# An encoder layer's output projection: by halves of 512 rows, seven products over the whole contraction, with sums of its weights made in the first pass

## The chip, the cores and the metric

The kernel runs on one core of a Trainium2 chip, as one program. The metric is the device time in microseconds (us), from three runs; what is compared is their median. One further execution was profiled. The engines are named as in the profile: PE is TensorE (PEld its weight loads), DVE VectorE, ACT ScalarE, POOL GpSimd, SP SyncE, which issues nearly all transfers in one queue, in order.

## The reference

One layer on x of 1024 rows by 2048 columns, in float32:

```python
h = rmsnorm(x, pre_g) * (1.0 + scale[:, None]) + shift[:, None]   # shift, scale, gate = silu(c) @ w_ada + b_ada
q, k, v, gate_a, u, gate_p = split(h @ w_in)                      # w_in 2048 x 4608
y_a = windowed_gqa(q, k, v, rel_table, sink) * silu(gate_a)       # 1024 x 1024
y_p = multiscale_pool(u, w_pool_grp, pool_scale) * silu(gate_p)   # 1024 x 1024
g_a, g_p = split(sigmoid(h @ w_merge + b_merge))                  # w_merge 2048 x 4096
merged = g_a * (y_a @ w_br_attn) + g_p * (y_p @ w_br_pool)        # 1024 x 2048
o = merged @ w_out                                                # w_out 2048 x 2048
out = x + gate[:, None] * rmsnorm(o, post_g)
```

The output projection is `merged @ w_out` with the last line.

## The kernel before, in words

Every float32 matmul is done as three: both operands are split in a high and a low part (`split`, lines 90 to 92: ACT copies the high part, DVE subtracts it to get the low one), and hi x hi, hi x lo and lo x hi are summed in PSUM. Operands lie with the contraction on the 128 partitions.

The big products go by Strassen's scheme in Winograd's form (`strassen`, lines 202 to 288). A block of four 128 x 512 results costs seven products, not eight, on sums of quarters: the moving side has B11, T3, T2, B21, T4, T1 and B22, the weights A11, S3, S2, A12, A22, S1 and S4. T and S are sums and differences. A *pair* is one call of `strassen`: seven products of twelve matmuls with 512 moving columns (line 227). Its PSUM banks are X, Z and V. ACT or DVE empties them into tiles p7, u2, u4 and c (lines 237, 265, 282; p7 is `p` in the profile), and `finish` takes each result block. `run` (line 313) steps through a pair and works off a list of side steps between the products; the last product of a pair is run inside the next one.

The stages, in the program's order: x is normalised and turned; pass 1 multiplies the first half of h's contraction with w_in and w_merge (first four pairs apart, then `pass1`, line 584; about 120 to 425 us for the pairs on w_in that have side steps which read w_ada for modulation and gate); pass 2 takes the second half, with attention and pooling between; two branch projections, b = 0 and b = 1 (loop from line 946); the output projection (from line 1012).

In a pair the weights come by `load_raws` (line 172 and on, the transfers at 179) into `raw` tiles of a pool of four, `wp`; whi and wlo, the split weights, have four buffers each. In the branch projections `fetch_gate` (972) loads a gate `gt` and applies the sigmoid, `finish` (984) multiplies each block by it. For b = 0 the block goes to memory (mp_d). For b = 1 the block of b = 0 is loaded and added, which makes m, the merged rows. The first eight 128-row tiles of the contraction of m stay in SBUF (`mr`), the others go to memory (m_d). The inputs y are tiles of a pool (`ysrc`) that is closed when b = 1 begins; the result tiles of b = 1 lie in the pool `ev4`, opened before `mr`.

The output projection has two parts. Four `out_pair`s (1068 to 1130) do the first half of the contraction by seven products, with 256 weight columns as the moving side (lines 1075, 1077, 1078); the four weight sums are made on DVE at that place; partial results go to memory (po_d). Then the second half of the contraction is done without the scheme, 512 columns at a time (lines 1164 to 1166), and each block gets its first sum from po_d, its sum of squares (ACT) and its scale (DVE, POOL); `finish_rows` (1190) puts x and the row's norm to it.

The order on each engine is set by the program's scheduler from the code's order and its waits; each engine then runs its list in that order. An instruction that waits holds all behind it on its engine.

## Time and profile before

| | |
|---|---|
| runs, median (lowest to highest) | 2163.88 us (2163.26 to 2164.78) |
| the profiled execution's own time | 2160.09 us |
| its span, first to last instruction | 2158.1 us |
| PE busy | 2121.3 us, 98% |
| DVE, ACT, POOL busy | 67%, 50%, 4% |
| output projection, first to last matmul | 1807.6 to 2149.6 us |
| granted PE clock over the span | 0.999 |
| transfers, mean | 190 GB/s |

A row of a group gives the line, engine, operation, output and inputs by name, shape, count, then busy time and mean ns of one, then idle time of the engine ahead of it and who ended it. A row of the timeline gives start, length, engine, line and what is done; in brackets the idle time ahead and its releaser. A row of the chain of waits gives start, length and what. A row of the waits view gives who waited for whom: us in total, times, longest. PE's pipelined matmuls overlap, so the mean ns of one is longer than the pitch.

### The profile page before, as it was taken

To read this page: it belongs to the slowest core of one execution; us is meant where nothing else is said; L and a number is where in the kernel's file an instruction comes from. 1 tells how busy PE (TensorE), PEld (TensorE's weight loads), DVE (VectorE), ACT (ScalarE), POOL (GpSimd) and SP (SyncE) were. 2 spreads that over 40 slices of the span, in tenths; PEclk is the share of its full clock that TensorE was granted. 3 is DMA by queue.
4 is the path that set the end of the run, shared out by engine and by line. 5 is a ranking of instruction groups with operands and counts; after the bars stand their busy time and mean duration, and the time that the engine had idled before them with its cause. 6 is when DMAs were issued, how large, how long until landed. Compare 5 with 4: busy or idle time off the path is not lost.

```text
span 2158.1 us, 29842 instructions
## 1 busy us (share of the span) xinstructions
PE 2121.3 (98%) x10335; PEld 1768.0 (82%) x10335; DVE 1449.1 (67%) x2558; ACT 1088.9 (50%) x2045; POOL 77.9 (4%) x113
## 2 busy tenths in 40 slices
PE   6999999999999999999999999999999999999998
PEld 3588888888888888888888888888788888999886
DVE  5786666665445767767777887657858878544456
ACT  5654444444474636677775333335546545444353
POOL 0000000000000000000000000000000000000363
PEclk9999999999999999999999999999999999999999
DMA  9985566664443355545545666755645654538455
GB/s 328 289 271 190 187 204 197 211 197 138 164 155 103 131 191 177 164 166 193 168 156 181 225 211 214 233 171 185 224 161 163 203 168 160 190 110 292 149 198 188
DMA packets 281655, 410.58 MB, mean 190 GB/s; under 512 B 21482, under 2 KB 158850, under 8 KB 281504
## 3 DMA queue, kind: packets, MB, share of 16 engines
q1 hardware_dynamic: 280048, 406.43, 57.4%
q0 software_dynamic: 1120, 2.19, 0.3%
q8 instruction: 81, 1.33, 0.3%
q14 instruction: 70, 0.57, 0.1%
q10 hardware_dynamic: 336, 0.06, 0.0%
HBM read 295.32 MB, written 115.37 MB: 190 GB/s over the span
## 4 chain that ended last, share of the span: by engine, by line
PE 89%; DVE 4%; DMA 3%; ACT 2%; issue 1%; SPq 0%; ACTq 0%; DVEq 0%
PE Z L227 29%; PE V L227 19%; PE X L227 19%; PE OUT L1166 3%; PE OUT L1165 3%; PE OUT L1164 3%; PE GEMV L444 1%; PE Z L1077 1%; PE Z L1078 1%; PE Z L1075 1%; DVE wlo L92 1%; PE XT L396 1%; DMA gt<-proj_d 1%; PE V L1078 1%; PE V L1075 1%
## 5 line engine op out<-in xcount | busy, mean ns | idle before, releaser
L91 ACT ACTIVATE whi<-raw 128x512 fp32r<-128x512 f32 (+1 forms) x584 | 356.2, 612 | 596.4 <-PE Z L227 279.6
L92 DVE TENSOR_TENSOR wlo<-raw,whi 128x512 fp32r<-128x512 f32 (+1 forms) x584 | 399.2, 687 | 292.0 <-PE Z L227 181.5
L95 DVE TENSOR_TENSOR u<-V,u 128x512 f32<-128x512 f32 x96 | 66.0, 688 | 53.3 <-PE V L227 48.2
L95 DVE TENSOR_TENSOR raw<-raw,raw 128x512 f32<-128x512 f32 x80 | 55.1, 688 | 61.9 <-DMA raw<-in_w_merge_dram 40.2
L227 PE MATMUL X<-B11h,whi 128*128 128x512 f32 x336 | 92.4, 393 | 1.3 <-ACT B11h L91 0.8
L227 PE MATMUL Z<-T1h,whi 128*128 128x512 f32 x336 | 92.1, 392 | 1.5 <-ACT T1h L91 1.5
L227 PE MATMUL V<-T4h,whi 128*128 128x512 f32 x336 | 92.3, 393 | 0.0
L227 PE MATMUL Z<-B22h,whi 128*128 128x512 f32 x336 | 92.2, 394 | 0.0
L227 PE MATMUL V<-T3h,whi 128*128 128x512 f32 x336 | 91.8, 392 | 0.0
L227 PE MATMUL X<-B11l,whi 128*128 128x512 f32 x336 | 91.3, 390 | 0.2 <-DVE B11l L92 0.2
L227 PE MATMUL Z<-T2h,whi 128*128 128x512 f32 x336 | 91.3, 391 | 0.0
L227 PE MATMUL X<-B21h,whi 128*128 128x512 f32 x336 | 90.9, 390 | 0.0
L227 PE MATMUL Z<-B22l,whi 128*128 128x512 f32 x336 | 90.9, 390 | 0.0
L227 PE MATMUL V<-T4l,whi 128*128 128x512 f32 x336 | 90.9, 390 | 0.0
L227 PE MATMUL Z<-T2h,wlo 128*128 128x512 f32 x336 | 90.9, 390 | 0.0
L227 PE MATMUL V<-T3l,whi 128*128 128x512 f32 x336 | 90.8, 390 | 0.0
L227 PE MATMUL V<-T4h,wlo 128*128 128x512 f32 x336 | 90.8, 390 | 0.0
L227 PE MATMUL Z<-T1l,whi 128*128 128x512 f32 x336 | 90.8, 390 | 0.0
L227 PE MATMUL Z<-T1h,wlo 128*128 128x512 f32 x336 | 90.7, 390 | 0.0
L227 PE MATMUL Z<-T2l,whi 128*128 128x512 f32 x336 | 90.7, 390 | 0.0
L227 PE MATMUL X<-B11h,wlo 128*128 128x512 f32 x336 | 90.6, 390 | 0.0
L227 PE MATMUL X<-B21l,whi 128*128 128x512 f32 x336 | 90.6, 390 | 0.0
(310 smaller groups left out, 5064.6 us busy)
## 6 DMA issues: line engine op xcount, KB each, us to landing
part<-part_d SPq DMA_DIRECT2D x136, 256.0 KB, 4.7
ada<-in_w_ada_dram SPq DMA_DIRECT2D x128, 256.0 KB, 4.4
raw<-in_w_in_dram SPq DMA_DIRECT2D x64, 512.0 KB, 4.0
raw<-in_w_merge_dram SPq DMA_DIRECT2D x64, 512.0 KB, 4.8
proj_d<-part SPq DMA_DIRECT2D x68, 256.0 KB, 2.1
gada<-in_w_ada_dram SPq DMA_DIRECT2D x32, 512.0 KB, 4.4
gt<-proj_d SPq DMA_DIRECT2D x64, 256.0 KB, 3.7
raw<-in_w_out_dram SPq DMA_DIRECT2D x32, 512.0 KB, 4.2
```

Source lines behind the costliest of these rows:

```text
L91: nc.scalar.activation(hi, src, AF.Copy)
L92: nc.vector.tensor_tensor(lo, src, f32(hi), ALU.subtract)
L95: (eng or nc.vector).tensor_tensor(o, a, b, ALU.add)
L227: nc.tensor.matmul(ps, w_[:, i], op[mov][j][m_], start=fresh and i == 0 and n == 0, stop=i == nj - 1 and n == 2, skip_group_check=True)
L396: nc.tensor.matmul(banks[j][:, m * P:(m + 1) * P], xts[4 * s + m, q][:, j * P:(j + 1) * P], turn[4 * s + m], start=True, stop=True)
L444: ins = nc.tensor.matmul(pv[g:g + 32, :], scz[:, kc, :], tile_of(kc), start=kc < 4, stop=kc >= 12, tile_position=(0, g))
L1075: nc.tensor.matmul(o_, hi[:, ts_], wh, start=fresh and t % 2 == 0 and j == 0, stop=False, skip_group_check=True)
L1077: nc.tensor.matmul(o_, hi[:, ts_], wl, start=False, stop=False, skip_group_check=True)
L1078: nc.tensor.matmul(o_, lo[:, ts_], wh, start=False, stop=j == KS - 1, skip_group_check=True)
L1164: nc.tensor.matmul(pb, hi[:, ts_], wh, start=fresh and k == KP[0], stop=False, skip_group_check=not fresh)
L1165: nc.tensor.matmul(pb, hi[:, ts_], wl, start=False, stop=False, skip_group_check=not fresh)
L1166: nc.tensor.matmul(pb, lo[:, ts_], wh, start=False, stop=k == KT - 1, skip_group_check=not fresh)
```

## The change

The output projection now goes by halves of 512 rows of x and, in each, by two blocks of 512 weight columns out of each half of w_out: four `out_pair`s of seven products over the whole contraction of 2048. Each product is 4 groups (JP) of 2 tiles, 2 banks (128 rows each), 3 matmuls: 48 matmuls, with 512 weight columns moving. The sums S1 to S4 of w_out's quarters are made during the first sixteen pairs of pass 1 (`weight_sums`: four loads of 256 KB with the pair's first product, four additions on DVE and four stores behind its sixth) and are stored in `ws_d`; the output projection loads them like plain weights. Result tiles in pass 1 go from 9 buffers to 6, and the sums have 6. In b = 1 the merged rows of half 0 stay in SBUF, those of half 1 go through m_d; `mr` is now opened before `ev4`, and `ev4` is closed before the output projection. The first half's first blocks go to memory (o_d). Work on half 0's rows is spread over the third and fourth `out_pair`; the last pair finishes rows 4 and 5 (of eight blocks of 128) behind its fifth product, and rows 6 and 7 at the end. POOL has no part in the stage.

```diff
@@ pass 1
+    ev = ev_ctx.enter_context(pool("ev1a", 6, side="right"))
+    wsp = ev_ctx.enter_context(pool("wsum", 6, side="right"))
...
+    def weight_sums(j, i):
+        a = {}
+        def fetch():
+            for name, kh, nh in (("11", 0, 0), ("21", 0, 1), ("22", 1, 1), ("12", 1, 0)):
+                a[name] = wsp.tile([P, 512], F32, tag="sw", name=uid("sw"))
+                n0 = nh * (D // 2) + i * 512
+                load(a[name], wo_rows(kh)[:, j, n0:n0 + 512])
+        def make():
+            s2 = wsp.tile([P, 512], F32, tag="sw", name=uid("sw"))
+            sub(a["21"], a["11"], a["21"])
+            sub(s2, a["22"], a["21"])
+            add(a["11"], a["11"], s2)
+            sub(a["12"], a["12"], s2)
+            for name, t in (("S3", a["21"]), ("S2", s2), ("S1", a["11"]), ("S4", a["12"])):
+                store(ws_rows(name)[:, j, i * 512:(i + 1) * 512], t)
+        return (0, fetch), (5, make)
...
+    sums = [weight_sums(j, n) for n in range(2) for j in range(KT // 2)]
+    pass1(-(-2 * len(side) // 7), side, EASY, sums)
@@ branch projection b = 1
-            ev = ctx.enter_context(pool("ev4", 4, side="right"))
-            mr = ctx.enter_context(pool("mraw", 4 * KS, side="right"))
+            mr = ctx.enter_context(pool("mraw", side="right"))
+            ev = ev_ctx.enter_context(pool("ev4", 4, side="right"))
...
-                    if i < KS:
-                        dst = mr.tile([P, 512], F32, tag="mraw", name=uid("mr"))
-                        m_t[2 * i + (blk[0] == "2"), int(blk[1]) - 1] = dst
+                    if blk[1] == "1":
+                        dst = mt[int(blk[0]) - 1][i // 2][:, i % 2]
...
-                    if i >= KS:
+                    if blk[1] == "2":
                         store(block(m_d, i * 256)(blk), dst)
@@ output projection: out_pair (256 columns), load_m, first_sums, evac, finish_rows go; new:
+    def weights(name, i, jp):
+        raw = wp.tile([P, 2, 512], F32, tag="raw", name=uid("wr"), bufs=4)
+        if name in ws_d:
+            load(raw, ws_rows(name)[:, 2 * jp:2 * jp + 2, i * 512:(i + 1) * 512])
+        else:
+            n0 = (name[1] == "2") * (D // 2) + i * 512
+            load(raw, wo_rows(int(name[2]) - 1)[:, 2 * jp:2 * jp + 2, n0:n0 + 512])
+        return raw
+    def out_mm(pb, op, name, jp, t, ws, first, last):
+        ts_ = slice(t * P, (t + 1) * P)
+        hi, lo = op[name][jp]
+        for x_, n in ((hi, 0), (lo, 0), (hi, 1)):
+            for jj in range(2):
+                nc.tensor.matmul(pb, x_[:, jj, ts_], ws[jj][n], ...)
+    def finish_block(T, n, scale):
+        r = held.pop((T, n))
+        nc.vector.scalar_tensor_tensor(r, r, scale, xrow.pop((T, n)), op0=ALU.mult, op1=ALU.add)
+        store(rows_of(T, n), r)
+    def out_pair(half, i, op, after):
...
+        product("S1", "T1", bz)
+        u4 = copies([slot("u4", F32) for _ in range(2)] if final else tiles("u4"), bz)
+        for t in range(2):
+            add(p7[t], p7[t], u4[t])
+            result("22", t, p7[t], p7[t])
+        after(5)
...
+        made = product("S4", "B22", bz, by_rows=True)
+        c12 = [slot("c12", F32) for _ in range(2)]
+        for t in range(2):
+            for jp in range(JP):
+                out_mm(bz[t], op, "B22", jp, t, made[jp], False, jp == JP - 1)
+            result("12", t, bz[t], c12[t])
+            scale = row_scale(6 + t)
+            for n in (0, 2, 3, 1):
+                finish_block(6 + t, n, scale)
...
+        if n == 4:
+            assert not side
+            for T in (4, 5):
+                scale = row_scale(T)
+                for b in range(4):
+                    finish_block(T, b, scale)
+    for half, i, after in ((0, 0, after_00), (0, 1, after_01), (1, 0, after_10), (1, 1, after_11)):
+        out_pair(half, i, ops[half], after)
```

(`result` squares the block on ACT with a sum per row, scales it on DVE and keeps or stores it.)

**ScalarE in the first pair of b = 1.** `p_..<-V` is the copy of bank V into p7; `T4h`, `T1h`, `B22h` are splits of the moving side, `gt` the gates' sigmoids. Before:

```order
L91 ACTIVATE T4h_15302<-y_14204 128x512
L91 ACTIVATE whi_15483<-raw_15370 128x512
L237 ACTIVATE p_3110_15412<-V_15376 128x512
L91 ACTIVATE T4h_15306<-y_14437 128x512
L976 ACTIVATE gt_15358<-gt_15358,cols 128x512
L91 ACTIVATE T4h_15310<-y_14642 128x512
L976 ACTIVATE gt_15361<-gt_15361,cols 128x512
L91 ACTIVATE T4h_15314<-y_14848 128x512
L976 ACTIVATE gt_15364<-gt_15364,cols 128x512
L91 ACTIVATE T1h_15318<-y_14159 128x512
L976 ACTIVATE gt_15367<-gt_15367,cols 128x512
```

and now:

```order
L91 ACTIVATE T1h_15602<-y_14443 128x512
L91 ACTIVATE T1h_15606<-y_14649 128x512
L91 ACTIVATE T1h_15610<-y_14882 128x512
L91 ACTIVATE whi_15826<-ws_15824 128x512
L91 ACTIVATE T1h_15614<-y_15087 128x512
L91 ACTIVATE B22h_15618<-y_14560 128x512
L91 ACTIVATE B22h_15622<-y_14765 128x512
L91 ACTIVATE B22h_15626<-y_14971 128x512
L91 ACTIVATE B22h_15630<-y_15204 128x512
L238 ACTIVATE p_3198_15704<-V_15668 128x512
L238 ACTIVATE u_3201_15724<-Z_15667 128x512
L1018 ACTIVATE gt_15650<-gt_15650,cols 128x512
```

The copy of V stood behind the first T4h; it now stands behind all T4h, T1h and B22h, and the gates behind it.

**VectorE in the last pair.** `wlo<-wr` are weights of product S1·T1, `L1116` the finishing of rows 4 and 5, now:

```order
L92 TENSOR_TENSOR wlo_19922<-wr_19919,whi_19921 128x512
L1116 SCALAR_TENSOR_TENSOR mo_18996<-mo_18996,st_19851,xr_19627 128x512
L1116 SCALAR_TENSOR_TENSOR c_4162_19731<-c_4162_19731,st_19851,xr_19629 128x512
L1116 SCALAR_TENSOR_TENSOR mo_18898<-mo_18898,st_19851,xr_19631 128x512
L1116 SCALAR_TENSOR_TENSOR u_4132_19619<-u_4132_19619,st_19851,xr_19633 128x512
L1111 RECIPROCAL st_19863<-st_19863 128x1
L92 TENSOR_TENSOR wlo_19926<-wr_19919,whi_19925 128x512
L1116 SCALAR_TENSOR_TENSOR mo_18996<-mo_18996,st_19863,xr_19635 128x512
L1116 SCALAR_TENSOR_TENSOR c_4163_19732<-c_4163_19732,st_19863,xr_19637 128x512
L1116 SCALAR_TENSOR_TENSOR mo_18898<-mo_18898,st_19863,xr_19639 128x512
L1116 SCALAR_TENSOR_TENSOR u_4133_19620<-u_4133_19620,st_19863,xr_19641 128x512
L92 TENSOR_TENSOR wlo_19944<-wr_19941,whi_19943 128x512
```

Eight finishing instructions stand between three low parts of one product.

**SP in pass 1.** `sw` are w_out's quarters, `ws_dS` the stored sums, `raw` the pair's weights, `part_d` its results, now:

```order
L180 DMA raw_2181<-in_w_in_dram 128x4x256
L304 DMA part_d<-p_470_1877 128x512
L180 DMA raw_2183<-in_w_in_dram 128x4x256
L616 DMA sw_2205<-in_w_out_dram 128x512
L616 DMA sw_2207<-in_w_out_dram 128x512
L616 DMA sw_2209<-in_w_out_dram 128x512
L616 DMA sw_2211<-in_w_out_dram 128x512
L410 DMA ada_2233<-in_w_ada_dram 128x2x256
L304 DMA part_d<-c_2078 128x512
L410 DMA ada_2233<-in_w_ada_dram 128x2x256
L410 DMA ada_2277<-in_w_ada_dram 128x2x256 x2
L625 DMA ws_dS_97<-sw_2207 128x512
```

Before, only `ada`, `part_d` and `raw` followed each other there; now four loads and four stores stand between a pair's weight loads and the next.

More of the change, by code (lines that the diff above doesn't have):

```diff
@@ L1182, in encoder_layer @@
[L1182 to L1194 removed]
+    merged_sums(mt, mt2, JP - 1)
```

425 lines of the change are left out of this document (194 added, 231 removed).

## The prediction

> **What bounds the kernel now.** I read the page's busy shares and its chain first, then what TensorE waited for, then the output projection as two stages.
>
> ```profile
> span 2158.1 us, 29842 instructions
> PE 2121.3 (98%) x10335; PEld 1768.0 (82%) x10335; DVE 1449.1 (67%) x2558; ACT 1088.9 (50%) x2045; POOL 77.9 (4%) x113
> PE 89%; DVE 4%; DMA 3%; ACT 2%; issue 1%; SPq 0%; ACTq 0%; DVEq 0%
> ```
>
> TensorE is busy 98% of the span and holds 89% of the chain, so a change pays by taking matmul time away and costs by every wait it puts on TensorE. The view of TensorE's waits, as far as it touches this change:
>
> ```profile
> PE Z L227 <- ACT T1h L91: 1.5, 2, 0.9
> PE V L1077 <- DVE wlo L92: 1.4, 1, 1.4
> PE X L1077 <- DVE wlo L92: 1.0, 1, 1.0
> PE Z L1077 <- DVE wlo L92: 0.5, 1, 0.5
> ```
>
> The three L1077 rows are the start of the output projection: 2.9 us in all. Its two halves in a table of windows (columns: window, length, PE busy (matmuls), granted clock, DMA share, GB/s), and a chain row of ordinary pairs:
>
> ```profile
> 1807.60:1974.75 167.15, 164.28 (x1357) 1.00 0.50 162
> 1974.75:2149.60 174.85, 174.85 (x770) 1.00 0.57 198
> 1807.60:2149.60 342.00, 339.13 (x2125) 1.00 0.54 180
> 2149.60:2158.10 8.50, 0.03 (x1) 0.66 0.58 217
> 1679.92 5.44 PE Z L227 x24
> ```
>
> The first window holds the seven-product half, 1344 matmuls of 256 moving columns (12 matmuls of the previous stage, L227, fall into it); the second holds 768 matmuls of 512 columns. A 512-column matmul takes 5.44/24 = 0.2267 us by the chain, 174.85/768 = 0.2277 by the window. A 256-column one takes (164.28 - 12 x 0.2267)/1344 = 0.1202 us. The clock is full, and there is no wait in the second window.
>
> **Term 1, the matmuls: -34.6 us.** The change replaces both halves by four pairs x seven products x 48 matmuls of 512 columns, again 1344 but wide. 1344 x 0.2267 = 304.7 us, with the 12 of the previous stage 307.4, against the 342.0 us (waits included) that the window holds now. The saving is that seven products now cover the whole contraction, not half of it.
>
> The Trainium skill (TensorE: Matmul & The Clock Gate, Back-to-back issue gap) gives an isolated gap of N/2.4 + 2.5 ns, 109 and 216 ns for the two widths; by it the estimate would be 312.5 us of matmuls before and 290.0 after, 22.5 saved. By it the whole sum would come to about 2160. The trace has 120 and 227 ns for the two in a stream without waits, so the trace decides.
>
> **Term 2, the start of the stage: +2.3.** The first product's weights now stand on VectorE behind seventeen instructions of the last branch pair's end, among them the gating that waits for that pair's last product. After that product come five VectorE instructions at a pitch of 0.6 us, about 3.1 us with the 0.68 of the first, and only some six matmuls (1.4 us) cover part of it; bounds 0 and 4, I take 2.3. The pitch is from rows of several instructions at once; the second row gives ScalarE's, 0.52, the third one split alone, the last two the finishing instruction (pitch 0.71) and the row sum of squares with its read-out:
>
> ```profile
> 1647.08 1.89 DVE L92 TENSOR_TENSOR T3l<-y,T3h 128x512 fp32r<-128x512 f32 x3
> 1646.77 1.14 ACT L91 ACTIVATE T3h<-y 128x512 fp32r<-128x512 f32 x2
> L91 ACT ACTIVATE whi<-raw 128x512 fp32r<-128x512 f32 x56 | 35.0, 627 | 65.4 <-PE OUT L1166 60.1 <-PE Z L1078 3.1 <-DMA raw<-in_w_out_dram 2.2
> 2151.81 1.42 DVE L1202 SCALAR_TENSOR_TENSOR o<-o,st,xr 128x512 f32<-128x512 f32 x2
> L1179 ACT ACTIVATION_READ_ACCUMULATOR jk<-o 128x1 f32 x28 | 5.2, 186 | 0.0
> L1179 ACT ACTIVATE jk<-o 128x512 f32<-128x512 f32 x28 | 17.4, 622 | 12.3 <-DVE o L95 12.3
> ```
>
> **Term 3, the end of the stage: +5.3.** In the last pair eight finishing instructions (4 x 0.71 + 0.16, then 4 x 0.71) stand between the weights of product S1·T1 on VectorE. A group of twelve matmuls lasts 2.72 us and the weights can be made two groups ahead; 5.8 us of foreign work less that cover leaves about 2.15. Then S4·B22 begins: ScalarE first empties both Z banks (the last copy ends about 0.2 + 0.6 us behind the last matmul), then splits the first weight (0.63): 1.45. Two sums of squares (0.62 + 0.19 each, and each behind an addition on VectorE) stand ahead of the second weight: about 1.7 more. Bounds: 0, if the waits of the order overlap, and 8. The tail behind the last matmul (8.5 us) has the same steps.
>
> The output projection so becomes 307.4 + 2.3 + 5.3 = 315 us: **-27.0**.
>
> **Term 4, the second branch projection: +8.3.** The pool of result tiles (`ev4`) is now opened behind the new `mr`, and lies over the inputs y. The timeline of the first pair, before:
>
> ```profile
> 1645.87 0.68 DVE L92 TENSOR_TENSOR T3l<-y,T3h 128x512 fp32r<-128x512 f32 x1
> 1662.68 0.60 ACT L237 ACTIVATE p<-V 128x512 f32<-128x512 f32 x1 [0.21 <-PE V L227]
> 1667.92 1.07 PE L227 MATMUL V<-T4h,whi 128*128 128x512 f32 x4
> 1672.13 0.50 PE L227 MATMUL Z<-T1h,whi 128*128 128x512 f32 x1 [0.64 <-ACT T1h L91]
> 1673.51 0.68 DVE L92 TENSOR_TENSOR B22l<-y,B22h 128x512 fp32r<-128x512 f32 x1
> 1645.15 4.18 DMA gt<-proj_d
> L987 DVE TENSOR_TENSOR c<-Z,gt 128x512 f32<-128x512 f32 x2 | 1.4, 681 | 0.0
> 1664.29 0.73 ACT L976 ACTIVATE gt<-gt,cols 128x512 f32<-128x512 f32 x1 [0.49 <-DMA gt<-proj_d]
> ```
>
> Now the copy of V to p stands on ScalarE behind all T4h, T1h and B22h, and it waits until the first B22l has read its y. Between T3l and that B22l stand as many VectorE instructions as before, so B22l ends near 1674.2 as now. The copy then runs to 1674.8 and the T4 product, which writes V, starts at 1674.95, not 1667.92: +7.0. The gates' loads wait for the last B22l (three pitches and 0.6 later, about 1676.6); 4.18 to land, 0.73 for the sigmoid and 0.68 for the multiplication free X at 1682.2, plus 0.2 for the signal (as much as V's copy idles behind V), when the next pair would want it at 1680.4: +1.95. The 0.64 that T1h costs now is hidden by this wait. 7.0 + 1.95 - 0.64 = 8.3; bounds 0, if the order bends, and 12. What is queued behind that copy on ScalarE is the copy of Z and four gates; TensorE waits for them too, within this count.
>
> **Term 5, the weight sums in pass 1: +2.** Sixteen pairs of 19.04 us (84 x 0.2267) each get four loads and four stores of 256 KB, 2.1 MB, and four VectorE instructions (4 x 0.6 = 2.4 us). Windows with all engines (length, PE, PEld, DVE, ACT, POOL busy, clock, DMA share, GB/s), and the stretch around one pair's second weight load:
>
> ```profile
> 45.00:50.00 5.00, 5.00 (x25) 1.64 (x25) 4.01 (x9) 3.71 (x7) 0.65 (x5) 1.00 1.10 348
> 120.00:130.00 10.00, 10.00 (x46) 8.29 (x45) 8.03 (x17) 4.97 (x11) 0.00 (x0) 1.00 0.95 333
> 300.00:400.00 100.00, 100.00 (x446) 82.81 (x446) 65.69 (x96) 41.27 (x67) 0.00 (x0) 1.00 0.61 199
> 1950.00:2000.00 50.00, 50.00 (x320) 45.64 (x320) 22.14 (x34) 22.21 (x42) 3.12 (x3) 1.00 0.92 310
> 247.72 0.37 SPq L179 DMA_DIRECT2D raw<-in_w_in_dram  x1
> 252.52 0.68 DVE L95 TENSOR_TENSOR raw<-raw,raw 128x512 f32<-128x512 f32 x1
> 253.65 0.63 ACT L91 ACTIVATE whi<-raw 128x512 fp32r<-128x512 f32 x1 [1.23 <-PE V L227]
> 257.08 1.07 PE L227 MATMUL Z<-T2h,whi 128*128 128x512 f32 x4
> ```
>
> 199 GB/s x 19.04 = 3.8 MB a pair; with 2.1 more it is 310 GB/s, at a share near 0.9. VectorE goes from 66% to 78%. The trace carries 333 GB/s at 0.95 without idle TensorE, so the throughput is there. What can suffer is latency: the weight needed for product T2 is ready at 254.3, 2.8 us before its product. SP's queue keeps order, and a store of a sum that waits for VectorE holds the weight load behind it. No cost is the lower bound; if all 2.1 MB (6.0 us at 348 GB/s) came ahead of that load, 3.2 us a pair, 51 us, is the upper. The 333 GB/s row is nearest, so I take 2.
>
> **Term 6, transfers of the output projection: +1.** A product loads four tiles of 512 KB; a pair loads 7 x 4 x 0.524 = 14.7 MB in 76.2 us, 193 GB/s. The third pair adds rows of x, earlier blocks and the output to some 21 MB, the fourth to some 24 MB, 315 GB/s. The 1950 to 2000 window carries 310 without idle TensorE, and a weight load issues about 9.6 us (four groups of 2.72 less the splits) ahead of its use where it takes
>
> ```profile
> raw<-in_w_out_dram SPq DMA_DIRECT2D x32, 512.0 KB, 4.2
> ```
>
> 4.2 us to land. Bounds 0 and 14 (below); I take 1. GpSimd's work and the `po_d` round trip go away; they lay beside TensorE (no wait on them in the waits view) and are worth nothing.
>
> **The sum**: -27.0 + 8.3 + 2 + 1 = -15.7 (rounded from -34.6 + 2.3 + 5.3 + 8.3 + 2 + 1). Span 2158.1 - 15.7 = 2142.4; the profiled execution's own time, 2160.1, lies 2.0 over its span and 3.8 under the runs' median of 2163.9; so 2163.9 - 15.7 = **2148 us**.
>
> **The rivals.**
> - *The gain in full* (0.17). The scheduler's order need not make TensorE idle where I count it: the copy of V may not be late (term 4) and the end may overlap (term 3). Then only -34.6 + 2.3: **2131.6**. For it: today's chain takes 2.9 us of waits in the whole stage. Against it: the copy's wait is on a tile that is read late by VectorE's order, and VectorE hardly idles there.
> - *Late transfers in the third and fourth pair* (0.17). If each of their 14 products waited 1 us on a weight, +14, less the 1 counted: **2161**. For it: 315 GB/s is above the 310 seen over 50 us. Against it: the 9.6 us lead.
> - *Slower: the weight load of pass 1 comes late* (0.12). It decides from 4.2 us on: less the 2.8 of slack that leaves 1.4 a pair, 22 us in sixteen, which eats the 17.7 that the other terms leave and 4.3 more. Halfway between that and the upper bound, 2.2 a pair: 35 us, -17.7 + 35 = +17, **2181**. For it: SP's stores stand between the weight loads (excerpt on SP). Against it: the 120 to 130 row.
>
> **How the numbers follow.** My forecast (2139 to 2156, bounds of terms 3 to 5 without their extremes) has 0.54. A change within 0.2% (4.3 us, 2159.5 to 2168.2) can't be told from none. Faster: 0.54 + 0.17 + 0.07 of the late transfers = 0.78. Slower: 0.10 of pass 1's rival + 0.01 of the late transfers = 0.11. The same: 0.11, the rest of these two. The range 2131 to 2166 holds the forecast, half of the full gain's own spread and most of the late transfers, and leaves pass 1's rival out.
>
> **What would show it.** Term 1: the new matmul line at 0.227 us each in windows without idle time, and a stage of 310 to 316 us from its first matmul to its last. Terms 2 and 3: waits of V or X on `wlo`, of Z on `wlo` and `wzh`, 2 us at the start, some 5 at the end. Term 4: TensorE idle for 7 us ahead of V<-T4h near 1668 (moved by what pass 1 does), released by the copy to p, and a shorter one at the next pair. Term 5: windows from 120 to 425 with 300 GB/s and the PE column within 1% of their length; `raw` or `whi` as a releaser in them would prove the slower rival. Term 6: no wait on `wr`. I am wrong in kind if the stage doesn't shrink by 25 us or more.

## The result, and the profile after

| | runs | median (lowest to highest) | ratio to before (95%) |
|---|---|---|---|
| before, runs taken beside it included | 6 | 2162.59 us (2156.06 to 2164.78) | |
| the change | 6 | 2175.87 us (2170.87 to 2178.1) | 1.0061 (1.0043 to 1.0079) |

The change makes the kernel slower by 0.6%. The forecast was 2148 us with 0.78 on faster: wrong in sign, and the time lies outside the range of 2131 to 2166. The page after, its span and busy shares:

```profile
span 2169.9 us, 28942 instructions
...
PE 2108.8 (97%) x9567; PEld 1719.6 (79%) x9567; DVE 1534.2 (71%) x2754; ACT 1123.0 (52%) x2124; POOL 7.5 (0%) x66
```

TensorE does 768 matmuls fewer (9567 for 10335), and its busy time falls by 12.5 us, yet the span grows by 11.8. The stages as windows from one stage's first matmul to the next one's (columns: window, length, PE busy (matmuls), granted clock, DMA share, GB/s), before:

```profile
100.00:837.97 737.97, 737.88 (x3317) 1.00 0.56 182
837.97:1488.47 650.50, 648.31 (x3119) 1.00 0.57 188
1488.47:1643.21 154.74, 153.36 (x673) 1.00 0.58 189
1643.21:1807.60 164.39, 163.75 (x721) 1.00 0.57 187
1807.60:2149.45 341.85, 338.98 (x2125) 1.00 0.54 181
```

and after:

```profile
100.00:852.48 752.48, 743.78 (x3317) 0.99 0.69 223
852.48:1505.92 653.44, 649.56 (x3119) 1.00 0.58 187
1505.92:1660.63 154.71, 153.41 (x673) 1.00 0.58 189
1660.63:1834.82 174.19, 167.52 (x722) 0.97 0.54 177
1834.82:2161.45 326.63, 315.33 (x1357) 0.99 0.78 256
```

From top to bottom: the passes up to attention +14.5, attention and pass 2 +2.9, the first branch projection 0, the second +9.8, the output projection -15.2. With 0.2 less behind the last matmul that is the span's +11.8. The forecast for the same rows was +2, 0, 0, +8.3 and -26. So the gain came in part, and pass 1, which does the same matmuls as before, ate it.

**Pass 1** loses its time in two windows (TensorE alone, same columns). Before:

```profile
280.00:320.00 40.00, 39.91 (x181) 1.00 0.58 189
320.00:425.00 105.00, 105.00 (x468) 1.00 0.59 192
425.00:470.00 45.00, 45.00 (x200) 1.00 0.69 225
```

After:

```profile
200.00:280.00 80.00, 80.00 (x359) 1.00 0.96 322
280.00:320.00 40.00, 35.86 (x153) 0.91 0.87 285
320.00:425.00 105.00, 105.00 (x468) 1.00 0.91 305
425.00:470.00 45.00, 40.44 (x163) 0.92 0.79 256
```

The 322 GB/s of the first row and the 305 of the third cost nothing: 468 matmuls in 105 us in both kernels. The second and fourth windows hold 28 and 37 matmuls fewer; 65 x 0.2267 = 14.7 us, which is all of the 14.5. Idle time makes 8.7 of it, and the granted clock of 0.91 and 0.92 most of the rest. TensorE's waits there, and what ended them:

```profile
PE PM L417 <- DVE acc L463: 4.1, 1, 4.1
PE V L228 <- DVE u L95: 2.6, 1, 2.6
PE Z L228 <- ACT u L238: 1.9, 1, 1.9
```

None of them names a weight. In the first two TensorE waits for an instruction of VectorE, in the third for a copy on ScalarE; none of the three depends on the sums of w_out. What VectorE itself waits for, between 120 and 560 us, and what SP's queue waits for ahead of the stores of the sums:

```profile
DVE sw L98 <- DMA sw<-in_w_out_dram: 16.9, 11, 3.8
DVE raw L95 <- DMA raw<-in_w_in_dram: 14.9, 8, 3.7
SPq L625 <- DVE sw L98: 31.3, 21, 3.6
```

In 11 of 64 additions VectorE stood still until the quarter of w_out had landed, with everything behind it in its list; and SP's queue stood at 21 of the stores until an addition was done, with every later transfer behind it. The trace does not tie one of TensorE's three waits to one such addition. Ahead of the first, VectorE waits 0.68 us for a quarter at 287.51 and 2.33 us for a weight of the pair at 286.13. The timeline of the second and of the third:

```profile
432.83 0.69 DVE L98 TENSOR_TENSOR ws<-raw 128x512 f32<-128x512 f32 x1 [1.82 <-DMA raw<-in_w_merge_dram]
...
433.44 0.68 DVE L95 TENSOR_TENSOR u<-V,u 128x512 f32<-128x512 f32 x1
...
434.18 1.20 PE L228 MATMUL V<-T3h,whi 128*128 128x512 f32 x4 [2.64 <-DVE u L95]
...
449.22 0.72 ACT L708 ACTIVATE xt<-xt,rstd 128x512 f32<-128x512 f32 x1 [1.74 <-DMA xt<-in_x_dram]
...
451.61 1.51 PE L228 MATMUL Z<-T1h,whi 128*128 128x512 f32 x4 [1.92 <-ACT u L238]
```

In the second, one of the pair's own weight sums (`ws`, not a sum of w_out) waits 1.82 us for a raw weight that lands late; the addition that empties V stands behind it, and TensorE, which wants V, idles for 2.64 us. Then come matmuls at half the pace: four of them, from 435.21 on, take 1.87 us, where four at 0.2267 end within about 1.1. VectorE comes to that place late: its longest wait for a quarter, 3.77 us, ends at 416.51, and it works without a pause from there to 431. In the third, ScalarE waits for rows of x, and the copy that empties Z stands behind them in its list.

**The second branch projection** (timeline):

```profile
1690.63 0.68 DVE L92 TENSOR_TENSOR B22l<-y,B22h 128x512 fp32r<-128x512 f32 x1
...
1691.35 0.60 ACT L238 ACTIVATE p<-V 128x512 f32<-128x512 f32 x1 [0.63 <-DVE B22l L92]
...
1691.99 2.07 PE L228 MATMUL V<-T4h,whi 128*128 128x512 f32 x4 [6.50 <-ACT p L238]
```

The copy of V waits until B22l has read its y, and TensorE waits 6.50 us for the copy: the step of term 4, with 7.0 forecast.

**The output projection** waits as follows:

```profile
PE X L1096 <- DVE wlo L92: 3.1, 3, 2.2
PE Z L228 <- ACT u L283: 2.5, 1, 2.5
PE Z L1096 <- ACT wzh L91: 2.5, 2, 1.5
PE Z L1096 <- DVE wlo L92: 2.2, 3, 1.0
```

Its 1356 matmuls would take 307.4 us at 0.2267; it took 326.4, so 19.0 went elsewhere. At the start, 11.7 us pass from its first matmul (1834.82) to the one at 1846.55, with 22 matmuls (5.0 us) between: 6.7. At the end, 16.4 us pass from 2144.84 to the last start at 2161.2 for 55 matmuls (12.5): 3.9. The other 8.4 lie in the middle, in short waits on wlo (3.0 us by the waits view) and the slower matmuls right behind them, such as those at 1909.76. The cause of that one stands on VectorE:

```profile
1908.41 0.69 DVE L98 TENSOR_TENSOR t<-m,m 128x512 f32<-128x512 f32 x1 [2.98 <-DMA m<-m_d]
1909.02 2.49 DVE L92 TENSOR_TENSOR wlo<-wr,whi 128x512 fp32r<-128x512 f32 x4
```

A sum for the next half's moving side waits 2.98 us for merged rows that are still on their way, with four weight splits behind it. In the third and fourth pair the finishing instruction does the same, and waits for rows of x:

```profile
L1116 DVE SCALAR_TENSOR_TENSOR mo<-mo,st 128x512 f32<-128x512 f32 x8 | 6.0, 752 | 18.0 <-DMA mo<-in_x_dram 15.4 <-DMA mo<-o_d 2.6
```

### The profile page after: what moved, and what is told of

It is laid out like the page before. It is cut to its first block, busy times and chain, and to the rows that moved or that the text cites. A ratio compares the mean times of both kernels' runs of the same rounds, so it can differ in the third digit from the quotient of the medians.

```text
span 2169.9 us, 28942 instructions
## 1 busy us (share of the span) xinstructions
PE 2108.8 (97%) x9567; PEld 1719.6 (79%) x9567; DVE 1534.2 (71%) x2754; ACT 1123.0 (52%) x2124; POOL 7.5 (0%) x66
## 5 line engine op out<-in xcount | busy, mean ns | idle before, releaser
L91 ACT ACTIVATE whi<-raw 128x512 fp32r<-128x512 f32 (+1 forms) x528 | 320.3, 610 | 507.6 <-PE Z L228 257.7
L92 DVE TENSOR_TENSOR wlo<-raw,whi 128x512 fp32r<-128x512 f32 (+1 forms) x528 | 347.1, 661 | 178.9 <-PE Z L228 119.0
L91 ACT ACTIVATE whi<-wr 128x512 fp32r<-128x512 f32 x216 | 125.5, 624 | 99.2 <-PE V L1096 32.8
L92 DVE TENSOR_TENSOR wlo<-wr,whi 128x512 fp32r<-128x512 f32 x216 | 139.4, 686 | 48.0 <-ACT whi L91 43.5
L1018 ACT ACTIVATE gt<-gt,cols 128x512 f32<-128x512 f32 x64 | 45.9, 723 | 108.3 <-DMA gt<-proj_d 91.7
L228 PE MATMUL V<-T3h,wlo 128*128 128x512 f32 x336 | 91.4, 392 | 0.0
L228 PE MATMUL Z<-B22h,wlo 128*128 128x512 f32 x336 | 91.2, 391 | 0.0
```

Of the source, the lines that this page charges most:

```text
L91: nc.scalar.activation(hi, src, AF.Copy)
L92: nc.vector.tensor_tensor(lo, src, f32(hi), ALU.subtract)
L228: nc.tensor.matmul(ps, w_[:, i], op[mov][j][m_], start=fresh and i == 0 and n == 0, stop=i == nj - 1 and n == 2, skip_group_check=True)
L1018: nc.scalar.activation(gt, gt, AF.Sigmoid, bias=cols[:, col:col + 1])
```

## The experiments

Times below are medians (lowest to highest) with the ratio to before and its interval; "pass 1" is the time of attention's first matmul less 837.97 us, that of before. Stage times come from the one profiled execution of a kernel, and the executions of one kernel lie 4 to 16 us apart. The first theory was the forecast's own parts with new sizes: pass 1 pays for a VectorE that is kept waiting by transfers, b = 1 for term 4, the output stage for its start, middle and end. The rival for pass 1 was the volume: 310 GB/s that the transfers don't carry without delay.

### The gates' pool ahead of the merged rows

```diff
-            mr = ctx.enter_context(pool("mraw", side="right"))
-            ev = ev_ctx.enter_context(pool("ev4", 4, side="right"))
+            ev = ctx.enter_context(pool("ev4", 4, side="right"))
+            mr = ctx.enter_context(pool("mraw", side="right"))
...
-    ev = ctx.enter_context(pool("ev5", side="right"))
```

The output stage then uses ev4's tiles.

> The changed kernel, but in the second branch projection the pool of result tiles (ev4) is opened ahead of mr, so that it lies where the closed pool of the first branch lay and not over the inputs y; it stays open and serves the output projection too (ev5 goes). Theory (overlap of buffers): the copy of V to p no longer waits for the first B22l. The idle 6.9 us ahead of the T4 product and the half-speed matmuls behind it (about 2.7 us) go: the stretch from T3h's split of y to the output projection shrinks by 9 to 10 us, and the time by 8 to 11 against the changed kernel, to about 2165. Rival (VectorE or the gates' loads hold the second projection anyway): the wait moves to another releaser and less than 4 us are won.

2163.75 us (2158.95 to 2167.15), 1.0006 (0.9993 to 1.0019). The wait of p is gone and b = 1 takes what it took before (TensorE alone; columns as above):

```profile
1663.16:1827.54 164.38, 164.19 (x722) 1.00 0.57 189
```

Term 4 is shown: the order of two lines costs 9.8 us. The other stages stay as they were in the change (pass 1 +15.1, output stage 327.6).

### What in the sums costs pass 1

Four kernels that leave work out. Without the sums, S1 to S4 replaced by a plain block of w_out of the same size:

```diff
-    pass1(-(-2 * len(side) // 7), side, EASY, sums)
+    pass1(-(-2 * len(side) // 7), side, EASY)
...
-            load(raw, ws_rows(name)[:, 2 * jp:2 * jp + 2, i * 512:(i + 1) * 512])
+            load(raw, w_out[0:D // 2, 0:D // 2].rearrange("(j p) n -> p j n", p=P)
+                 [:, 2 * jp:2 * jp + 2, i * 512:(i + 1) * 512])
```

> The changed kernel without weight sums in pass 1 (no loads, additions or stores of them); the output projection loads blocks of w_out in their place, which leaves the sums out of the result but keeps every load and matmul of that stage. Theory (the sums cost pass 1 its 14.5 us): attention begins at about 838 us as before the change instead of 852.5, and the time falls by 13 to 18 us, to about 2160. Rival (the loss comes from the smaller pool of result tiles in pass 1, 6 instead of 9): attention still begins at 848 or later.

2157.97 us (2154.66 to 2161.8), 0.998 (0.997 to 0.9989); pass 1 -0.3, so all of the 14.5 is the sums', and none of it the smaller pool of result tiles. With the loads and stores alone, the quarters stored as they are (the additions left out):

```diff
-            sub(a["21"], a["11"], a["21"])
-            sub(s2, a["22"], a["21"])
-            add(a["11"], a["11"], s2)
-            sub(a["12"], a["12"], s2)
```

> The changed kernel with the loads and the stores of the weight sums in pass 1 but without the four additions on VectorE: the loaded blocks are stored as they are, so the sums are left out of the result. Theory A (transfers: SP's queue and later landings make VectorE wait, and the splits behind it): pass 1 still loses 10 us or more, attention begins at 848 or later. Theory B (VectorE's own time): most of it is won back, attention begins at 842 or earlier, time about 2163.

2164.44 us (2157.04 to 2170.02), 1.0007 (0.9993 to 1.0022); pass 1 +4.3. With the additions alone, on tiles that stay in SBUF (no load or store, and a plain block of w_out as above):

```diff
         def fetch():
-            for name, kh, nh in (("11", 0, 0), ("21", 0, 1), ("22", 1, 1), ("12", 1, 0)):
...
+            a.update(still)
```

> The changed kernel with the four additions on VectorE in sixteen pairs of pass 1, but on five tiles that stay in SBUF, without loads and stores; the output projection loads blocks of w_out, so the sums are left out of the result. Theory A (transfers): pass 1 loses 3 us or less, attention begins at 841 or earlier, time about 2161 to 2164. Theory B (VectorE's own time): pass 1 loses 10 us or more, attention begins at 848 or later. If both this and the run without additions lose little, it takes both together.

2160.57 us (2156.68 to 2164.96), 0.9994 (0.9984 to 1.0004); pass 1 +1.1. The two alone make 5.4, not 14.5: it is neither the volume alone nor VectorE's 64 additions alone, but something between the two. With both, but the additions on one resident tile that waits for no load (and the quarters stored as they are, so that no store waits for an addition; five tiles for the quarters, not six):

```diff
-            sub(a["21"], a["11"], a["21"])
+            sub(still, still, still)
...
```

> The changed kernel with all loads and stores of the weight sums and also four additions on VectorE at their places, but the additions work on one tile that stays in SBUF: nothing on VectorE waits for the loaded blocks. The sums are left out of the result. Theory (in-order waiting: the cost comes from additions that wait on VectorE for late loads, with the splits for TensorE behind them): pass 1 loses about the sum of the two parts, 1.4 + 4.6, attention begins at 842 to 846, time about 2165 to 2168. Rival (plain load: VectorE and the transfers are both fuller, no matter who waits for whom): attention begins at 850 or later, time about 2175.

2170.45 us (2163.3 to 2179.13), 1.004 (1.0026 to 1.0053); pass 1 +9.6. The additions' wait for their quarters, and with it the stores' wait for the additions, makes 4.9 of the 14.5. TensorE's three waits are still there at their places, 1.9, 2.3 and 1.6 us. Of the other 9.6, 4.2 are more than the two parts alone, although no addition of a sum waits for a load there. VectorE's waits for raw weights (between 120 and 560 us) grow too, to 58.0 us in four rows (21.9, 14.6, 10.9 and 10.6), where the kernel without sums has 16.2; such a wait only costs where something that TensorE needs stands behind it. So the theory "VectorE waits for the quarters" holds a third of the cost at most. The medians rank the four kernels of this part the same way: in the order shown they lie 17.9, 11.4, 15.3 and 5.4 us under that of the change.

### The additions on another engine, the stores in another queue

On top of the first experiment, the four additions on GpSimd:

```diff
-            sub(a["21"], a["11"], a["21"])
+            g_ = nc.gpsimd.tensor_tensor
+            g_(a["21"], a["11"], a["21"], ALU.subtract)
...
```

> The run with ev4 ahead of mr, and the four additions of each weight sum made on GpSimd instead of VectorE; loads and stores as before, result complete. Theory (in-order waiting on VectorE): GpSimd waits for the blocks, VectorE doesn't, so pass 1 loses what the transfers alone cost: attention begins at 841 to 845 instead of 853, time 8 to 12 us under the run with ev4 ahead, about 2152 to 2156. Rival (SP's queue: stores that wait for sums hold the weight loads whoever makes them): attention still begins at 849 or later, time about 2162.

2184.26 us (2179.51 to 2185.52), 1.0097 (1.0081 to 1.0112): a miss, pass 1 +34.6. Groups of this kernel (line, engine, operation, tiles, count | busy, mean ns | idle ahead):

```profile
L624 POOL TENSOR_TENSOR sw<-sw,sw 128x512 f32<-128x512 f32 x16 | 26.9, 1680 | 7.0 <-DMA sw<-in_w_out_dram 7.0
L463 DVE SCALAR_TENSOR_TENSOR acc<-ada,sc,acc 128x512 f32<-128x512 f32 x60 | 57.5, 959 | 0.4
```

and the second of them in the change:

```profile
L463 DVE SCALAR_TENSOR_TENSOR acc<-ada,sc,acc 128x512 f32<-128x512 f32 x60 | 44.7, 745 | 1.1 <-DMA ada<-in_w_ada_dram 0.9
```

One addition takes 1.68 us on GpSimd, and while it runs VectorE's own instructions are slower, 959 ns for 745 in the mean (the 43 of the 60 that no addition of GpSimd overlaps keep 745); TensorE waited 16.9 us for acc alone. The Trainium skill (GPSIMD Engine Reference, Specifications) says that GpSimd shares its SBUF interfaces with VectorE and contends with instructions that have two SBUF inputs; these rows agree.

The stores of the sums by GpSimd's queue, with the first experiment and the mends of the next part:

```diff
-                store(ws_rows(name)[:, j, i * 512:(i + 1) * 512], t)
+                nc.gpsimd.dma_start(ws_rows(name)[:, j, i * 512:(i + 1) * 512], t)
```

> The combined run with the additions back on VectorE and the stores of the weight sums issued from GpSimd's queue instead of SP's; loads stay on SP; result complete. Theory (SP's in-order queue: a store that waits for its sum holds the weight loads of the pair and of modulation behind it): pass 1 loses 2 to 7 us instead of 15, attention begins at 840 to 845; with the stage at 316 the time is 2143 to 2149. Rival (VectorE waits for the late blocks in its own order, whatever stores them): attention still begins at 849 or later, time about 2153.

2174.75 us (2171.81 to 2179.59), 1.006 (1.0041 to 1.008): a miss, pass 1 +35.2. In the waits of SP's queue the loads now stand behind the buffers that the stores still read:

```profile
SPq L616 <- DMA ws_dS<-sw: 29.9, 22, 3.1
```

The same wait in the change is 0.9 us. How much of the 35.2 it makes isn't shown.

### The output stage mended

Three mends. MID: the finishing of half 0's blocks gets its rows three steps ahead in place of two, and the merged rows of the next half, from which the sums of its moving side are made, are asked for at products 5 and 6, one product earlier. END: rows 4 and 5 are finished behind the weights of the last product, which are made ahead of the copies of Z. START: the first two groups of A11's weights are split ahead of b = 1's last blocks.

```diff
-            for a_, b_ in zip(todo, todo[2:]):
+            for a_, b_ in zip(todo, todo[3:]):
...
-        if n == 6:
+        if n == 5:
             nextm.extend(merged_tiles())
-            fetch_merged(nextm, 0)
+        if n >= 5:
+            fetch_merged(nextm, n - 5)
...
-        if n == 4:
-            assert not side
+        if n == 6:
             for T in (4, 5):
...
+        if final:
+            made = product("S4", "B22", bz, by_rows=True)
         u4 = copies([slot("u4", F32) for _ in range(2)] if final else tiles("u4"), bz)
...
+    early_ws.append(first_group(1))
     merged_sums(mt, mt2, JP - 1)
```

The first experiment with MID and END:

> The run with ev4 ahead of mr, and in the output projection: the merged rows of half 1 are fetched one product earlier, the blocks of half 0 are fetched three ahead instead of two, the finishing of rows 4 and 5 comes behind the weights of S4, and these weights are split ahead of the copies of Z. Theory (VectorE's in-order waits and the end's order cost 6 us in the middle and 3 to 4 at the end): the stage shrinks from 327.6 to 318 to 321 us, time about 2155. Rival (the transfers themselves are too slow there): the waits on wlo in the third and fourth pair stay, the stage stays above 324.

2155.59 us (2150.89 to 2164.44), 0.9974 (0.9952 to 0.9995). The output stage:

```profile
1826.22:2143.44 317.22, 312.05 (x1356) 0.99 0.79 263
```

327.6 to 317.2 at the same bytes: the waits in the middle and at the end came of when the rows were asked for and of where they stood in VectorE's list, not of a lack of transfer. Two windows of its third and fourth pair:

```profile
2001.00:2041.00 40.00, 39.93 (x176) 1.00 0.94 320
2041.00:2081.00 40.00, 39.82 (x174) 1.00 0.97 330
```

At 320 and 330 GB/s they hold 176 and 174 matmuls, where a window without waits holds 178; in the change three windows hold 166 and 167 at 283 to 308 GB/s. With START and the additions on GpSimd:

> All of it in one: ev4 ahead of mr, additions on GpSimd, the middle and the end as in the run before, and the first two groups of weights of the output projection made ahead of the last merged block. Theory: the gains add up, pass 1 -9, start -4, middle and end -8 against the run with ev4 ahead (2163.8): about 2143, a stage of 314 to 317 us, faster than the kernel before the change by 18 us or more. Rival (the stage is held by the transfers): the stage stays above 322 and the time above 2149.

2173.77 us (2170.84 to 2176.53), 1.0052 (1.0036 to 1.0068); output stage 315.5, pass 1 +36. With START, no sums (a plain block of w_out as above):

> The mended kernel without any weight sums in pass 1, blocks of w_out loaded in their place, so the sums are left out of the result. It shows what is left of the gain when pass 1 pays nothing. Theory (terms add up): attention begins at 838, the stage takes 316 to 318, time 2136 to 2140, that is 24 us under before less about 3 us that pass 2 has lost in every version. Rival (pass 1's delay hid work that now waits elsewhere): the stage or the second projection grows and the time stays above 2144.

2139.98 us (2137.48 to 2142.09), 0.9893 (0.9878 to 0.9908); output stage 319.4. So the idea of the change, with the mends, is worth 1.1% where pass 1 pays nothing. START shows no gain: the stage takes 315.5 to 321.6 in the eight kernels of all that have it, 317.2 without.

### The sums spread over more pairs

All with the first experiment, MID, END and START. Sixteen sums over 22 pairs, in place (S2 written over a quarter, four tiles a sum), by the code's order alone:

```diff
-        return (0, fetch), (5, make)
+        return fetch, make, keep
...
+    for n, (f_, m_, k_) in enumerate(sums):
+        at7 = n * 7 * first // len(sums) - (n == len(sums) - 1)
+        for d, step in ((1, f_), (6, m_), (8, k_)):
+            q = min(at7 + d, 7 * first - 1)
+            place[q // 7].append((q % 7, step))
```

> The combined run with additions on VectorE, and the sixteen weight sums spread evenly over the 22 pairs of pass 1: loads one product after a sum's start, additions five products later, stores two products after that, all on SP's queue. Theory (what counts is that an instruction in SP's or VectorE's order finds its data there): the waits get rarer, pass 1 loses 4 to 9 us, attention begins at 842 to 847, time 2144 to 2151. Rival (the sum of transfers counts): 16 sums are 16 sums, attention at 850 or later, time about 2153.

2165.44 us (2158.85 to 2167.65), 1.0012 (1.0001 to 1.0023): a miss, pass 1 +27.2, with 13.8 us of waits for acc. The group shows that the sums were hardly spread (duration, then first and last start):

```profile
L98 DVE TENSOR_TENSOR sw<-sw,sw x48: 675/686/694, 164.2 to 443.5; 128x512 f32<-128x512 f32 x48
```

In the change the same group runs from 164.1 to 427.3. Where the code places the sums up to near 560 us, the scheduler drew them forward, to end at 443.5. Why that costs 12.7 us more than in the change isn't shown. The same with the stores on GpSimd's queue:

> Both of the last two runs: sums spread over 22 pairs, stores from GpSimd's queue. Theory: both waits go, pass 1 loses 1 to 5 us, attention begins at 839 to 843, time 2140 to 2146. Rival: no better than the better one of the two, because the loads' landing alone costs the 4.6 us that the run without additions showed.

2182.51 us (2178.39 to 2188.08), 1.0096 (1.0072 to 1.012), pass 1 +46: both misses at once. Half of the sums in the last eight pairs, in steps of 256 columns with smaller pools there (the other half over the 22 pairs before):

```diff
+        steps_ = [weight_sums(j, n, c0, 256) for c0 in range(0, 512, 256)]
...
-    ev = ev_ctx.enter_context(pool("ev1b", 6, side="right"))
+    ev = ev_ctx.enter_context(pool("ev1b", 5, side="right"))
+    wsp = ev_ctx.enter_context(pool("wsum1b", 4, side="right"))
```

> The mended kernel (ev4 ahead of mr, middle, end and start of the output projection changed, additions on VectorE, stores on SP) with only eight of the sixteen weight sums in the first 22 pairs of pass 1, one in every 2.75 pairs with the additions a pair behind the loads; the other eight are made in half-width steps in the last eight pairs of pass 1, where the transfers' share was 0.35 to 0.5, with 5 instead of 6 result tiles and 3 instead of 4 x tiles there. Result complete. Theory (sums and the loads of w_ada meet in the same queues; apart they cost little): attention begins at 839 to 844, the stage takes 316 to 318, time 2138 to 2145, faster than the kernel before by some 20 us. Rival (every sum costs its share, 0.9 us, wherever it is made): attention at 850 or later, time about 2153.

2163.85 us (2157.55 to 2168.61), 1.0009 (0.9998 to 1.0019), pass 1 +22; TensorE's waits name u again, now among the last pairs (12.2 us in two waits).

### The order held

What was left to try was the order itself. Every load, addition and store of the sums is held where the code has it, and nothing else is changed:

```diff
-                load(a[name], wo_rows(kh)[:, j, n0:n0 + 512])
+                tc.keep_in_program_order(load(a[name], wo_rows(kh)[:, j, n0:n0 + 512]))
...
+                tc.keep_in_program_order(nc.vector.tensor_tensor(o_, x_, y_, f_))
...
-                store(ws_rows(name)[:, j, i * 512:(i + 1) * 512], t)
+                tc.keep_in_program_order(store(ws_rows(name)[:, j, i * 512:(i + 1) * 512], t))
```

> The changed kernel with one edit: the loads, additions and stores of the weight sums are held in the order of the code; places, buffers, second projection and output projection as in the changed kernel. Theory (order): attention begins at 840 to 843 instead of 852.5, the other stages stay (second projection 174, output projection 326), time about 2163 to 2166. Rival (the pins only help together with the other edits): attention begins at 848 or later, time 2171 or more.

2164.1 us (2159.88 to 2166.86), 1.0013 (1.0003 to 1.0022); pass 1 +5.2 in place of +14.5. Its additions:

```profile
L622 DVE TENSOR_TENSOR sw<-sw,sw x64: 681/684/693, 168.2 to 466.9; 128x512 f32<-128x512 f32 x64
```

and as a row of the page's kind of groups (busy, mean ns | idle ahead):

```profile
L622 DVE TENSOR_TENSOR sw<-sw,sw 128x512 f32<-128x512 f32 x64 | 42.5, 685 | 0.3
```

The same instructions on the same engine, one step a pair as written: 299 us for the sixteen sums, where the free order ran through them in 263, and VectorE idles 0.3 us for them, not 16.9. SP's queue waits 17.5 us for the sums that it stores, 1.2 us at most, where it waited 34.0 with 3.6 at most. In the windows of TensorE, the one at 425 is free again and the one at 280 loses less:

```profile
280.00:320.00 40.00, 37.40 (x162) 0.96 0.85 280
...
425.00:470.00 45.00, 45.00 (x200) 1.00 0.95 320
```

The bytes are the same and at 425 they run at 320 GB/s without loss. 9.3 of the 14.5 us are order; the 5.2 that stay are close to the 4.3 of the transfers alone. The waits for u are gone, and the rows of x that held ScalarE are asked for from 476 us on, not from 439; TensorE's wait for acc stays, 4.2 us in three. How long VectorE waits in all is no measure of the cost: its waits for the pairs' own weights are 69.1 us here and 35.8 in the change. The same with the first experiment, MID, END and START:

> The same with the sums at the changed kernel's places, one per pair in the first sixteen pairs, loads with the first product, additions and stores behind the sixth, all held in the order of the code. Theory (order): pass 1 loses 3 to 8 us, attention begins at 841 to 846. Rival (the rate of one sum per pair, 2.1 MB on 19 us, is too much whatever the order): attention at 850 or later; then the run that is spread should be better by as much as the rate is lower.

2146.23 us (2141.31 to 2150.44), 0.9936 (0.9917 to 0.9955), pass 1 +2.9. And with the sums spread over 22 pairs as in the section before, but held there:

> The mended kernel with all sixteen weight sums in pass 1, on VectorE and SP, spread evenly over the 22 pairs, and every load, addition and store of them held in the order of the code (behind what the code issues earlier on its engine). Without that the scheduler had drawn the sums forward: in the run meant to spread them they came every 17.8 us, as in the changed kernel (17). Result complete. Theory (order: additions placed early in VectorE's order by the scheduler wait there for late loads, and the splits for TensorE behind them): pass 1 loses 1 to 6 us, attention begins at 839 to 844, time 2140 to 2147, faster than before by 15 us or more. Rival (the load as such, each sum its share): attention at 850 or later, time about 2153.

**2140.8 us** (2136.2 to 2143.29), 0.9908 (0.9891 to 0.9925): faster than before by 0.9% and than the change by 1.6%, with nothing left out. The kernel that was to spread the sums differs from this one in the held order alone: pass 1 goes from +27.2 to +1.6. Its first and last stage (TensorE alone):

```profile
100.00:839.60 739.60, 737.87 (x3315) 1.00 0.69 226
...
1811.73:2130.30 318.57, 312.29 (x1357) 0.99 0.80 264
```

Pass 1 +1.6, attention and pass 2 +3.3, b = 1 -0.7, the output stage -23.0. The sums end at 566 us here, the windows of pass 1 need 250 to 280 GB/s and the wait for acc is 0.4 us, although VectorE waits 10.9 us for quarters. Against the sums held in place, spreading takes 1.3 us off pass 1, and the output stage, which it doesn't edit, is 3.0 shorter; the executions of the two kernels overlap, so what spreading itself is worth stays open.

## Why the prediction was wrong

The sum missed by 27.5 us of span (-15.7 forecast, +11.8 measured): 12.5 in pass 1, 10.8 in the output stage, 2.9 in attention, 1.5 in b = 1, less 0.2 at the tail.

- **Term 1, the matmuls, was right.** A wide matmul of the new line has a pitch of 0.2267 us wherever TensorE does not wait, and 768 instructions went. But the stage's length was 326.4, not 315: the test named for it (310 to 316) failed by the terms around it.
- **Term 5, the weight sums: the step that failed.** Forecast +2, measured +14.5. The reading of throughput was right (305 and 322 GB/s without loss). What failed was "no cost is the lower bound ... the 333 GB/s row is nearest": I took the order as the code has it and looked only for a late weight load. The order that was issued ran the sums ahead of their pairs, VectorE, ScalarE and SP's queue stood at transfers or sums that were not there yet, and the modulation's sums and the emptying of V and Z came late behind them. Holding the order takes 9.3 of the 14.5 away, and 25.6 of 27.2 where the sums are to be spread. Which of the lists matters most stays open, since loads, additions and stores were held at once; by the kernel with the resident tile, the additions' wait for quarters and the stores' wait for additions make 4.9 together.
- **The slower rival** had the right sign at 0.12. Its mechanism, a late load in every pair, is only half of what happened: loads are late, but it shows in three waits in sixteen pairs, two by way of VectorE and one by ScalarE, and `raw` or `whi` is not named as a releaser of TensorE. Its 22 us to decide weren't reached either; 14.5 sufficed because the other terms gave less. (Halfway between 1.4 and 3.2 us a pair is 2.3, not 2.2: 37 us and 2183.)
- **Term 4 was right in place, cause and nearly in size**, 9.8 for 8.3. The wait is 6.50 (7.0 forecast). The second, that of the gates (1.95), does not appear; in its place some 14 matmuls behind the wait ran at half pace, 14 x 0.2 = 2.8.
- **Term 2, the start, was mis-sized**: 6.7 for 2.3. Beside the wait for wlo (2.2) there is one of Z for the copy of the previous product (2.5), which stands on ScalarE behind the new stage's splits. I had asked for VectorE's list alone.
- **Term 3, the end**: 3.9 for 5.3, with the steps that were named (wlo 0.5, then wzh 1.5 and 1.0). Its first step was mis-sized in the working: 5.8 us less two groups of 2.72 leaves 0.4, not 2.15, and 0.5 came.
- **Term 6 was mis-sized, and its cause was another**: 8.4 in the middle for 1. No wait on `wr` shows, as forecast; but VectorE waits for m and x rows in its list and holds the weight splits. The rival of late transfers came nearer in size (14) with the wrong transfers: not the weights, which were asked for early enough, but rows that come late into an engine's list. MID and END, which move the steps of the middle and the end only, give 10.4 back.
- **Attention and pass 2, +2.9, was not forecast, and stays open.** It is there without any sums (653.9 in the second experiment) and in the best version (653.8). The waits are of about 1 us each, on tiles of ScalarE and VectorE. In the sixteen kernels of the experiments, none of which edits this stage, it takes from 651.4 us (additions on GpSimd, with all mends) to 658.2 (the resident tile), where before has 650.5.

## What to carry to other kernels

Where each engine runs a list in order, an instruction that is off the critical path but waits for a transfer is not free: price it by what stands behind it in its list, not by how long it waits, and read the order that is really issued, not the one written. Hidden work should be held at its place. Here the same 64 additions and 34 MB of transfers cost 14.5 us in the free order and 5.2 held in place; in the mended kernel they cost 27.2 where the free order was to spread them, 2.9 held in place, and 1.6 held and spread. And a pool that is opened in another order is a change of waits: the order of two lines was worth 9.8 us.

## What the runs showed of the hardware

TensorE runs at half pace for a while behind some waits. The windows of 5 us around the first stall of the change (TensorE alone):

```profile
290.00:295.00 5.00, 3.26 (x15) 1.00 0.96 314
295.00:300.00 5.00, 2.60 (x10) 0.53 0.97 327
300.00:305.00 5.00, 5.00 (x19) 0.79 0.39 129
```

Behind the idle 4.1 us the granted clock is 0.53 and the pitch 0.427 us, for some microseconds. In the change the same pitch shows behind idle times of 6.5, 2.6, 2.5 and 1.9 us, for 6 to 14 matmuls; behind 0.7 to 1.5 us at most two matmuls are slow, and no more behind 2.2 us at 1846. The length alone does not decide: with the order held alone, 3.27 us of idle time ahead of 1835.01 leave the granted clock at 1.00, and in the kernel with the sums held and spread 1.85 us ahead of 2117.91 are followed by seven matmuls at 0.427. So a wait of about two microseconds or more can cost up to 3 us more than itself; in pass 1 the slow matmuls behind the three waits cost about 4.5 us. The Trainium skill (TensorE: Matmul & The Clock Gate, Part 1: The HAM clock gate) gives 426.7 ns for a cold matmul of this width, as here, and at least one idle window of about 3.4 us before it goes cold; the rows with 1.9 to 2.6 us show less than that to be enough.
